# Weight sums and differences of a seven-product down projection, formed on GpSimd instead of VectorE

## The chip, the cores and the metric

The kernel runs on one core of one Trainium2 chip. The metric is the time of one execution on the device in microseconds; the kernel before takes 2917.14 us (median of 3 runs, 2915.57 to 2918.15). All names and lines below are those of the kernel before.

## The reference, cut to what matters

One decoder layer on 512 tokens of width 2048, in float32: three token mixers, a gated merge, an output projection and a squared-ReLU MLP of width 8192. The change lies in the second matrix product of the MLP:

```python
h2 = rms_norm(x, mlp_norm_w[l])
x = x + jnp.square(jax.nn.relu(h2 @ w_mlp_up[l])) @ w_mlp_down[l]
```

`w_mlp_down` is 8192 x 2048 in float32.

## The kernel before, in words

**Matrix products in three passes.** A float32 tile is split into a high part, rounded to the type that TensorE multiplies (fp32r), and the rest. `wsplit` (lines 110 to 115) does that for a weight tile `raw` of 128 partitions x 1024 elements: ScalarE casts it to `whi` (L112), then VectorE subtracts to get `wlo` (L114). `mm3` (lines 122 to 125) issues three matmuls for each product: high with high, high with rest, rest with high. There are four buffers for `raw` (`RAWS = 4`) and three each for `whi` and `wlo`.

**The MLP in eight slices.** The 8192 hidden channels go in eight slices of 1024 (`NE = 8`). For a slice, `up_steps` forms the hidden activations `u` (accumulators `fa`): 16 weight tiles, 24 matmuls each. `down_units` multiplies them with the slice's rows of `w_mlp_down` and adds the result into `x1` (accumulators `da`). For seven of the eight slices it does so by seven products of quarter matrices instead of eight (Strassen's scheme, the table `SEVEN`): each product takes one quarter or a sum or difference of two quarters of the activations, the same of the weights, and its result is added to one or two quarters of the output (L1001, on VectorE, reading `da` from PSUM). Of the seven products five take a sum or difference of two weight quarters, in the table's order the first three and the last two; the fourth and fifth take one quarter as it is.

**The step.** `merged_order` alternates one step of the next slice's up projection with one step of this slice's down projection. A step of the pair, as the text calls it, is thus one up tile (called U; 24 matmuls) and one down unit: half the columns of one product, which is two weight tiles (called A and B here, `i = 0` and `i = 1`; 12 matmuls each). A slice has 14 such steps: 6 with paired weights, 4 with single ones, 4 with paired ones; the two up tiles left over follow, so that three up tiles stand in a row there. Seven slices have 70 steps with paired weights, and 140 sums.

**A paired weight tile.** Both quarters come by DMA into two `raw` buffers (L988, 512 KB each, queue of SyncE). L991 adds the second to the first in place; then the tile goes through `wsplit`:

```python
for k0, m0, _ in bt:
    raw = wp.tile([P, 2, 512], F32, tag="raw", bufs=RAWS, name="raw")
    nc.sync.dma_start(out=raw, in_=rows(w_dn, e_ * 1024 + k0 * 512 + i * 256, m0 * 1024 + c * 512, 512))
    raws.append(raw)
if len(bt) == 2:
    nc.vector.tensor_tensor(out=raws[0], in0=raws[0], in1=raws[1], op=sgn[bt[1][2]][0])
hi, lo = wsplit(raws[0], 512)
```

The second buffer of a pair is free when the sum is done, the first when `wlo` is. A paired step so takes five `raw` buffers of a ring of four: one for U (L104), two for A, two for B. SyncE issues the transfers in the order U, A, A, B, B; each waits until its buffer has been read.

**The order of the work.** Each engine runs its instructions in a fixed order that a scheduler sets when the program is built; an instruction that waits holds all behind it on its engine or queue.

Of the kernel before, what the change touches and what calls it, by code (L numbers as in the profile page):

```python
# [49 lines left out]
def tile_layer(ctx: ExitStack, tc: tile.TileContext, a, out: bass.AP):  # L50
    nc = tc.nc
# [9 lines left out]
    def T(name, dt=F32, shape=(P, 512)):  # L61
        return big.tile(list(shape), dt, tag="T", bufs=N_SLOTS, name=name)
# [4 lines left out]
    def sm(name, shape=(P, 512)):  # L67
        return psm.tile(list(shape), F32, tag="sm", name=name)
# [41 lines left out]
    def wsplit(raw, n):  # L110
        hi = wp.tile([P, 2, n], F32R, tag="whi", bufs=3, padded_shape=[P, 2, 512], name="whi")
        nc.scalar.copy(out=hi, in_=raw)  # L112
        lo = wp.tile([P, 2, n], F32R, tag="wlo", bufs=3, padded_shape=[P, 2, 512], name="wlo")
        nc.vector.tensor_tensor(out=lo, in0=raw, in1=hi.bitcast(F32), op=ALU.subtract)  # L114
        return hi, lo

    def rows(w, k0, c0, n):
        return w[k0:k0 + 2 * P, c0:c0 + n].rearrange("(k p) c -> p k c", p=P)
# [3 lines left out]
    def mm3(ps, l_hi, l_lo, r_hi, r_lo, first, last):  # L122
        nc.tensor.matmul(ps, lhsT=l_hi, rhs=r_hi, start=first, stop=False)  # L123
        nc.tensor.matmul(ps, lhsT=l_hi, rhs=r_lo, start=False, stop=False)  # L124
        last_mm[0] = nc.tensor.matmul(ps, lhsT=l_lo, rhs=r_hi, start=False, stop=last)  # L125
# [721 lines left out]
    for h in range(NH):  # L847
# [3 lines left out]
        raws = []  # L851
# [85 lines left out]
    sgn = {1: (ALU.add, r2), -1: (ALU.subtract, nr2)}  # L937
# [24 lines left out]
    def split(src):  # L962
        hh = T("a_h", F32R, (P, 2, 256))
        hl = T("a_l", F32R, (P, 2, 256))
        nc.scalar.copy(out=hh, in_=src)  # L965
        nc.vector.tensor_tensor(out=hl, in0=src, in1=hh.bitcast(F32), op=ALU.subtract)
        return hh, hl

    def down_units(e_, u):

        for at, bt, ct in SEVEN:
            act = []
            for i in range(2):
                t0, k0, _ = at[0]
                src = u[2 * k0 + i, t0]
                if len(at) == 2:
                    t1, k1, s1 = at[1]
                    both = T("a_s", shape=(P, 2, 256))
                    nc.vector.tensor_tensor(out=both, in0=src, in1=u[2 * k1 + i, t1], op=sgn[s1][0])
                    src = both  # L980
                act.append(split(src))
            for c in range(2):
                accs = [sm("da") for _ in range(2)]
                for i in range(2):
                    raws = []
                    for k0, m0, _ in bt:
                        raw = wp.tile([P, 2, 512], F32, tag="raw", bufs=RAWS, name="raw")
                        nc.sync.dma_start(out=raw, in_=rows(w_dn, e_ * 1024 + k0 * 512 + i * 256, m0 * 1024 + c * 512, 512))  # L988
                        raws.append(raw)
                    if len(bt) == 2:  # L990
                        nc.vector.tensor_tensor(out=raws[0], in0=raws[0], in1=raws[1], op=sgn[bt[1][2]][0])  # L991
                    hi, lo = wsplit(raws[0], 512)
                    ah, al = act[i]
                    for t in range(2):
                        for k in range(2):
                            cs = slice(t * P, (t + 1) * P)
                            mm3(accs[t], ah[:, k, cs], al[:, k, cs], hi[:, k, :], lo[:, k, :], i == 0 and k == 0, i == 1 and k == 1)
                for t in range(2):
                    for t0, m0, s0 in ct:
                        tt, cc_ = 2 * t0 + t, 2 * m0 + c  # L1000
                        nc.vector.scalar_tensor_tensor(out=x1[tt, cc_], in0=accs[t], scalar=sgn[s0][1][:, tt:tt + 1], in1=x1[tt, cc_], op0=ALU.mult, op1=ALU.add)  # L1001
                yield
# [12 lines left out]
    for e_ in range(NE - 1):  # L1015
        nu = {}
        merged_order(up_steps(e_ + 1, nu), down_units(e_, u))
        u = nu
# [81 lines left out]
```

## Time and profile before

| what | value |
|---|---|
| median of 3 runs | 2917.14 us (2915.57 to 2918.15) |
| profiled execution: its own time | 2913.22 us |
| profiled execution: span of the instructions | 2911.4 us |
| granted TensorE clock, mean | 0.998 of full speed |
| TensorE busy with matmuls | 2880.4 us, 99% of the span |
| VectorE busy | 1569.0 us, 54% |
| ScalarE busy | 1016.0 us, 35% |
| GpSimd busy | 125.1 us, 4% |

The profiled execution's own time is 1.8 us over its span. Shares of busy time are means over stages with different limits; the MLP with the seven products lies from about 1667 to 2808 us, and there the shares are others. Idle time of an engine costs something only where TensorE comes to wait for it.

### The profile page before, as it was taken

Reading aid. Unit: us, or ns where it says so; the run is one execution under the profiler, and the core shown is the slowest. Engines: PE = TensorE matmul, PEld = TensorE weight load, DVE = VectorE, ACT = ScalarE, POOL = GpSimd, SP = SyncE. Lnnn points to the kernel's source line nnn. Section 1 sums busy time; section 2 is a strip of 40 time slices with the busy share of each in tenths; the row PEclk is TensorE's granted clock in tenths of the full one; section 3 lists DMA queues with packets and bytes.
Section 4 is the critical chain, followed back from the end, with each engine's and each line's share of the span. In section 5 each row is a group of like instructions: output and inputs, shape, how many; then the busy total and the mean of one; then the engine's idle time right before and its main releaser. Section 6 shows DMA issues by size and latency. Waiting matters only on the chain.

```text
span 2911.4 us, 34617 instructions
## 1 busy us (share of the span) xinstructions
PE 2880.4 (99%) x13710; PEld 2341.0 (80%) x13710; DVE 1569.0 (54%) x2194; ACT 1016.0 (35%) x1606; POOL 125.1 (4%) x134
## 2 busy tenths in 40 slices
PE   8999999999999999999999999999999999999999
PEld 6988777777888888888888888787888878788887
DVE  5435665645223233333332377767777677777753
ACT  6333434334222222222232333333434333343431
POOL 0001111100000010000000000000000000000000
PEclk9999999999999999999999999999999999999999
DMA  6423222222333333333333366656666666656653
GB/s 230 115 73 89 68 64 71 57 56 59 101 94 97 99 94 101 95 95 100 123 110 103 120 210 209 212 181 209 192 204 204 208 217 196 209 184 210 192 181 109
DMA packets 259773, 403.47 MB, mean 139 GB/s; under 512 B 23159, under 2 KB 80282, under 8 KB 259610
## 3 DMA queue, kind: packets, MB, share of 16 engines
q1 hardware_dynamic: 250240, 398.61, 44.3%
q10 hardware_dynamic: 9370, 2.64, 0.4%
q8 instruction: 107, 1.75, 0.2%
q14 instruction: 56, 0.46, 0.1%
HBM read 396.60 MB, written 4.60 MB: 138 GB/s over the span
## 4 chain that ended last, share of the span: by engine, by line
PE 87%; DVE 5%; DMA 5%; ACT 1%; issue 1%; POOL 1%; SPq 0%; ACTq 0%; DVEq 0%; POOLq 0%
PE fa L123 19%; PE fa L125 19%; PE fa L124 19%; PE da L124 6%; PE da L125 6%; PE da L123 5%; DMA raw<-in_w_mlp_down_dram 4%; PE ta L123 2%; PE ta L124 2%; PE ta L125 2%; DVE wlo L114 2%; DVE raw L991 2%; DVE x L1001 1%; PE dps L807 1%; PE ps L814 1%
## 5 line engine op out<-in xcount | busy, mean ns | idle before, releaser
L114 DVE TENSOR_TENSOR wlo<-raw,whi 128x1024 fp32r<-128x1024 f32 (+2 forms) x604 | 723.2, 1205 | 909.5 <-ACT whi L112 906.4
L112 ACT CAST whi<-raw 128x1024 fp32r<-128x1024 f32 (+2 forms) x604 | 621.9, 1035 | 1434.6 <-PE fa L124 709.2
L123 PE MATMUL fa<-h_h,whi 128*128 128x512 f32 x2336 | 928.0, 397 | 0.0
L125 PE MATMUL fa<-h_h,wlo 128*128 128x512 f32 x2336 | 913.6, 391 | 2.7 <-DVE wlo L114 2.6
L124 PE MATMUL fa<-h_l,whi 128*128 128x512 f32 x2336 | 912.8, 391 | 0.0
L123 PEld LDWEIGHTS fa<-h_h,whi 128*128 128x128 f32 x2336 | 438.8, 188 | 97.9 <-issue 11.3
L125 PEld LDWEIGHTS fa<-h_h,wlo 128*128 128x128 f32 x2336 | 438.7, 188 | 97.2 <-DVE wlo L114 5.3
L124 PEld LDWEIGHTS fa<-h_l,whi 128*128 128x128 f32 x2336 | 439.1, 188 | 86.6 <-issue 1.2
L124 PE MATMUL da<-wlo,a_h 128*128 128x512 f32 x912 | 358.9, 393 | 7.9 <-DVE wlo L114 7.8
L123 PE MATMUL da<-whi,a_h 128*128 128x512 f32 x912 | 355.4, 390 | 0.2
L125 PE MATMUL da<-whi,a_l 128*128 128x512 f32 x912 | 355.1, 390 | 0.0
L991 DVE TENSOR_TENSOR raw<-raw 128x1024 f32<-128x1024 f32 x140 | 171.2, 1223 | 174.2 <-DMA raw<-in_w_mlp_down_dram 174.0
L124 PEld LDWEIGHTS da<-wlo,a_h 128*128 128x128 f32 x912 | 171.2, 188 | 54.5 <-DVE wlo L114 19.7
L123 PEld LDWEIGHTS da<-whi,a_h 128*128 128x128 f32 x912 | 171.3, 188 | 36.9 <-ACT a_h L965 1.0
L125 PEld LDWEIGHTS da<-whi,a_l 128*128 128x128 f32 x912 | 171.3, 188 | 34.4
L1001 DVE SCALAR_TENSOR_TENSOR x<-da,r,x 128x512 f32<-128x512 f32 x280 | 195.7, 742 | 0.2 <-PE da L125 0.2
L123 PE MATMUL ta<-whi,m_h 128*128 128x512 f32 x256 | 99.9, 390 | 0.0
L125 PE MATMUL ta<-whi,m_l 128*128 128x512 f32 x256 | 99.7, 389 | 0.0
L124 PE MATMUL ta<-wlo,m_h 128*128 128x512 f32 x256 | 99.7, 389 | 0.0
L123 PE MATMUL fa<-ob_h,whi 128*128 128x512 f32 x256 | 99.6, 389 | 0.0
L124 PE MATMUL fa<-ob_l,whi 128*128 128x512 f32 x256 | 99.6, 389 | 0.0
L125 PE MATMUL fa<-ob_h,wlo 128*128 128x512 f32 x256 | 99.6, 389 | 0.0
(286 smaller groups left out, 2114.2 us busy)
## 6 DMA issues: line engine op xcount, KB each, us to landing
raw<-in_w_mlp_down_dram SPq DMA_DIRECT2D x352, 512.0 KB, 4.1
raw<-in_w_mlp_up_dram SPq DMA_DIRECT2D x128, 512.0 KB, 3.8
raw<-in_w_in_dram SPq DMA_DIRECT2D x112, 512.0 KB, 3.6
raw<-in_w_in_dram SPq DMA_DIRECT2D x120, 256.0 KB, 3.0
raw<-in_w_out_dram SPq DMA_DIRECT2D x32, 512.0 KB, 3.8
raw<-in_w_mem_kv_dram SPq DMA_DIRECT2D x16, 512.0 KB, 4.2
raw<-in_p_swa_dram SPq DMA_DIRECT2D x12, 512.0 KB, 3.8
raw<-in_p_dn_dram SPq DMA_DIRECT2D x12, 512.0 KB, 3.9
```

What stands on the lines that cost most here:

```text
L112: nc.scalar.copy(out=hi, in_=raw)
L114: nc.vector.tensor_tensor(out=lo, in0=raw, in1=hi.bitcast(F32), op=ALU.subtract)
L123: nc.tensor.matmul(ps, lhsT=l_hi, rhs=r_hi, start=first, stop=False)
L124: nc.tensor.matmul(ps, lhsT=l_hi, rhs=r_lo, start=False, stop=False)
L125: last_mm[0] = nc.tensor.matmul(ps, lhsT=l_lo, rhs=r_hi, start=False, stop=last)
L807: nc.tensor.matmul(dps[rs, :], lhsT=R[rs, t, :], rhs=tmp, start=True, stop=True)
L814: nc.tensor.matmul(ps2, lhsT=kd[rs, t, :], rhs=delta, start=True, stop=True)
L991: nc.vector.tensor_tensor(out=raws[0], in0=raws[0], in1=raws[1], op=sgn[bt[1][2]][0])
L1001: nc.vector.scalar_tensor_tensor(out=x1[tt, cc_], in0=accs[t], scalar=sgn[s0][1][:, tt:tt + 1], in1=x1[tt, cc_], op0=ALU.mult, op1=ALU.add)
```

## The change

L991, the sum or difference of two weight tiles, is issued on GpSimd instead of VectorE. Operands, shapes and order in the program's text stay.

```diff
--- before.py
+++ after.py
@@ -988,7 +988,7 @@
                         nc.sync.dma_start(out=raw, in_=rows(w_dn, e_ * 1024 + k0 * 512 + i * 256, m0 * 1024 + c * 512, 512))
                         raws.append(raw)
                     if len(bt) == 2:
-                        nc.vector.tensor_tensor(out=raws[0], in0=raws[0], in1=raws[1], op=sgn[bt[1][2]][0])
+                        nc.gpsimd.tensor_tensor(out=raws[0], in0=raws[0], in1=raws[1], op=sgn[bt[1][2]][0])
                     hi, lo = wsplit(raws[0], 512)
                     ah, al = act[i]
                     for t in range(2):
```

On GpSimd all 140 sums stand in a row at the end of its program, behind the merge's last additions:

```order
 L894 TENSOR_TENSOR mg<-mg,sg 128x512 x32
+L991 TENSOR_TENSOR raw<-raw 128x1024 x140
 L1096 UNCONDITIONAL_BRANCH
```

Nothing else is issued there in the MLP, so a sum waits on GpSimd only for its own data.

On VectorE, in the paired steps late in a slice, the sums stood between the subtractions and the additions to `x1`. `wlo_15950` and `wlo_15971` are the rests of an A and a B tile, `wlo_15991` that of the next U:

```order
-L991 TENSOR_TENSOR raw_15943<-raw_15943,raw_15945 128x1024
+L114 TENSOR_TENSOR wlo_15950<-raw_15943,whi_15948 128x1024
 L1001 SCALAR_TENSOR_TENSOR x1_11397<-da_15865,r2_11993,x1_11397 128x512
-L114 TENSOR_TENSOR wlo_15950<-raw_15943,whi_15948 128x1024
 L1001 SCALAR_TENSOR_TENSOR x1_11399<-da_15866,r2_11993,x1_11399 128x512
-L991 TENSOR_TENSOR raw_15964<-raw_15964,raw_15966 128x1024
 L114 TENSOR_TENSOR wlo_15971<-raw_15964,whi_15969 128x1024
-L991 TENSOR_TENSOR raw_16031<-raw_16031,raw_16033 128x1024
 L114 TENSOR_TENSOR wlo_15991<-raw_15987,whi_15989 128x1024
```

The sums are gone from the row, and the subtractions keep their order among themselves.

On the queue of SyncE the transfers keep their order, and some waits change the engine whose counter they watch. 15943 and 15945 are the two quarters of an A tile, 15964 and 15966 those of its B tile, 15987 the next U, 16031 and 16033 the next A:

```order
-L988 DMA raw_15943<-in_w_mlp_down_dram 128x2x512 [waits DMAHW1_49,DVE_49]
+L988 DMA raw_15943<-in_w_mlp_down_dram 128x2x512 [waits DMAHW1_49,Pool_49]
 L988 DMA raw_15945<-in_w_mlp_down_dram 128x2x512 [waits DVE_49]
 L988 DMA raw_15964<-in_w_mlp_down_dram 128x2x512 [waits DVE_49]
-L988 DMA raw_15966<-in_w_mlp_down_dram 128x2x512 [waits DMAHW6_49,DMAHW2_49,DVE_49]
-L104 DMA raw_15987<-in_w_mlp_up_dram 128x2x512 [waits DMAHW4_49,DVE_49]
-L988 DMA raw_16031<-in_w_mlp_down_dram 128x2x512 [waits DMAHW0_49,DVE_49]
-L988 DMA raw_16033<-in_w_mlp_down_dram 128x2x512 [waits DMAHW6_49,DVE_49]
+L988 DMA raw_15966<-in_w_mlp_down_dram 128x2x512 [waits DMAHW6_49,DMAHW4_49,Pool_49]
+L104 DMA raw_15987<-in_w_mlp_up_dram 128x2x512 [waits DMAHW2_49,DVE_49]
+L988 DMA raw_16031<-in_w_mlp_down_dram 128x2x512 [waits DMAHW6_49,DMAHW0_49,Pool_49]
+L988 DMA raw_16033<-in_w_mlp_down_dram 128x2x512 [waits DVE_49]
```

The second quarter of B and the first quarter of the next A now wait for a sum on GpSimd (`Pool_49`); the second quarter of A stands right behind the first and waits for a subtraction.

## Rows read from the trace of the kernel before

**Rows 1.** The page, busy time of each engine.
```profile
PE 2880.4 (99%) x13710; PEld 2341.0 (80%) x13710; DVE 1569.0 (54%) x2194; ACT 1016.0 (35%) x1606; POOL 125.1 (4%) x134
```
**Rows 2.** Windows, the MLP's paired stage: PE, PEld, DVE, ACT, POOL busy, clock, DMA.
```profile
1667.00:2808.00 1141.00, 1130.34 (x4946) 925.08 (x4945) 841.30 (x939) 425.02 (x552) 0.00 (x0) 1.00 0.64 203
```
**Rows 3.** Groups of instructions in that stage: busy, mean ns, idle before.
```profile
L114 DVE TENSOR_TENSOR wlo<-raw,whi 128x1024 fp32r<-128x1024 f32 x305 | 367.7, 1220 | 125.7 <-ACT whi L112 124.2
...
L112 ACT CAST whi<-raw 128x1024 fp32r<-128x1024 f32 x303 | 315.7, 1052 | 610.9 <-DVE raw L991 389.8 <-PE fa L124 126.7 <-PE da L125 82.5
...
L991 DVE TENSOR_TENSOR raw<-raw 128x1024 f32<-128x1024 f32 x137 | 167.6, 1223 | 160.8 <-DMA raw<-in_w_mlp_down_dram 160.7
```
**Rows 4.** Waits in that stage: total us, times, longest.
```profile
DVE raw L991 <- DMA raw<-in_w_mlp_down_dram: 160.7, 102, 3.7
...
PE da L124 <- DVE wlo L114: 7.8, 10, 1.3
```
**Rows 5.** Waits of SyncE's DMA queue in that stage.
```profile
SPq L988 <- DVE raw L991: 106.4, 94, 1.7
```
**Rows 6.** Timeline of VectorE, four paired steps: start, length, what, idle before.
```profile
2099.59 1.23 DVE L991 TENSOR_TENSOR raw<-raw 128x1024 f32<-128x1024 f32 x1 [1.80 <-DMA raw<-in_w_mlp_down_dram]
...
2118.88 1.23 DVE L991 TENSOR_TENSOR raw<-raw 128x1024 f32<-128x1024 f32 x1 [2.36 <-DMA raw<-in_w_mlp_down_dram]
...
2124.14 1.23 DVE L991 TENSOR_TENSOR raw<-raw 128x1024 f32<-128x1024 f32 x1 [0.29 <-DMA raw<-in_w_mlp_down_dram]
...
2130.28 1.23 DVE L991 TENSOR_TENSOR raw<-raw 128x1024 f32<-128x1024 f32 x1 [2.50 <-DMA raw<-in_w_mlp_down_dram]
...
2151.62 1.23 DVE L991 TENSOR_TENSOR raw<-raw 128x1024 f32<-128x1024 f32 x1 [3.60 <-DMA raw<-in_w_mlp_down_dram]
```
**Rows 7.** Timeline of SyncE's queue beside them.
```profile
2120.14 0.37 SPq L988 DMA_DIRECT2D raw<-in_w_mlp_down_dram  x1
...
2122.56 0.37 SPq L988 DMA_DIRECT2D raw<-in_w_mlp_down_dram  x1
...
2125.39 0.37 SPq L988 DMA_DIRECT2D raw<-in_w_mlp_down_dram  x1
```
**Rows 8.** Timeline of TensorE: first matmuls of steps (`fa`) and of a down unit (`da`).
```profile
2100.29 0.39 PE L123 MATMUL fa<-h_h,whi 128*128 128x512 f32 x1
...
2111.17 0.39 PE L123 MATMUL fa<-h_h,whi 128*128 128x512 f32 x1
...
2160.13 0.39 PE L123 MATMUL da<-whi,a_h 128*128 128x512 f32 x1
```
**Rows 9.** Timeline of VectorE, early paired steps of another slice.
```profile
1867.16 1.22 DVE L991 TENSOR_TENSOR raw<-raw 128x1024 f32<-128x1024 f32 x1 [1.49 <-DMA raw<-in_w_mlp_down_dram]
...
1878.17 1.23 DVE L991 TENSOR_TENSOR raw<-raw 128x1024 f32<-128x1024 f32 x1 [1.33 <-DMA raw<-in_w_mlp_down_dram]
```
**Rows 10.** Timeline of TensorE there: first matmuls of two steps.
```profile
1867.23 0.39 PE L123 MATMUL fa<-h_h,whi 128*128 128x512 f32 x1
...
1878.38 0.39 PE L123 MATMUL fa<-h_h,whi 128*128 128x512 f32 x1
```
**Rows 11.** The `raw` tile's view in that stage, transfers from issue to landing.
```profile
DMA to landing us min/median/max: 3.6/4.1/6.1
```
**Rows 12.** GpSimd's groups over the whole span: busy, mean ns.
```profile
L701 POOL TENSOR_TENSOR craw<-craw,cc 128x256 f32<-128x256 f32 x6 | 4.4, 726 | 0.0
```
**Rows 13.** Timeline of GpSimd in the merge, two additions of the same shape.
```profile
1205.94 1.29 POOL L894 TENSOR_TENSOR mg<-mg,sg 128x512 f32<-128x512 f32 x1 [53.80 <-DVE sg L893]
...
1211.34 2.26 POOL L894 TENSOR_TENSOR mg<-mg,sg 128x512 f32<-128x512 f32 x1
```
**Rows 14.** Timeline of VectorE beside the second of them.
```profile
1210.15 0.68 DVE L893 TENSOR_TENSOR sg<-fa,sg 128x512 f32<-128x512 f32 x1
1210.76 1.71 DVE L114 TENSOR_TENSOR wlo<-raw,whi 128x1024 fp32r<-128x1024 f32 x1
1212.38 2.60 DVE L899 TENSOR_TENSOR m_l<-mg,m_h 128x512 fp32r<-128x512 f32 x2
```

## The prediction

> **What bounds the kernel now.** I read the page first: TensorE is busy 99% of the span [rows 1], so a change can only cost or give back what TensorE waits. The windows narrow that to the stage of the change, 1141 us in which VectorE is busy 841.30 us (74%), GpSimd not at all, and TensorE idles 1141.00 - 1130.34 = 10.7 us [rows 2]. That is about all there is to win.
>
> Then I asked what TensorE is close to waiting for. The groups of VectorE show that the sums (L991, 1.22 us each) sit idle 160.8 us before them, waiting for weights [rows 3]: 102 of the 137 sums that the trace holds there come as soon as their data land [rows 4]. The queue's waits show the other half: 94 times a transfer waits for a sum to free its buffer [rows 5]. Sum and transfer wait for each other: a loop. The timelines let one measure it. The sum of an A tile starts at 2118.88 and is done at 2120.11 [rows 6]; at 2120.14 SyncE issues the second quarter of B into the buffer that it freed [rows 7]; the sum of B starts at 2124.14, ends at 2125.37, and at 2125.39 the second quarter of the next A leaves, whose sum starts at 2130.28 [rows 6, 7]. One turn is 11.40 us: two sums (2.46) and two transfers with their handoffs (4.03 and 4.91). In the early steps of another slice it is 1878.17 - 1867.16 = 11.01 us [rows 9]. I take 11.2.
>
> TensorE needs 2111.17 - 2100.29 = 10.88 us for a step [rows 8]. So the loop is already a little slower than TensorE in paired steps. It hardly shows, because the tiles are ahead at the start of a run of paired steps and the lead is used up slowly; where it is used up the steps stretch to the loop (11.15 us, from the starts of two steps) [rows 10].
>
> **The change, part by part.**
>
> *Taken from VectorE:* 140 sums of 1.22 us, 171 us, and their waiting at the head of VectorE's row. Worth little: VectorE delays TensorE by a few us in all (7.8 us in ten waits for `wlo`) [rows 4].
>
> *Put on GpSimd:* 140 sums of 128x1024. The trace has no such shape on GpSimd. The nearest rows: 0.73 us for 128x256 [rows 12] and 1.29 us for 128x512 with nothing beside it [rows 13], so 0.56 us for every 256 more, and 1.29 + 2 x 0.56 = 2.41 us. Bounds: 1.22 us would need a GpSimd as fast as VectorE, which the 1.29 us for half the size rules out, so the lower end is the slope's 2.41 too; the upper one is twice 1.29 = 2.58. I take 2.41, from the slope of two rows.
>
> The Trainium skill puts a price on it too: "GPSIMD Engine Reference", section on performance versus the Vector engine, gives 4497 ns on GpSimd and 2293 ns on VectorE for 2048 elements; half of that, an estimate, is 2.25 us. By it the loop below is 0.32 us shorter and the time 3030 us; no run here shows that size.
>
> *The loop:* both its sums grow by 2.41 - 1.22 = 1.19, so 11.2 + 2.38 = 13.6 us. Nothing hides this: a sum starts when its data land and its end releases the next transfer. The queue's order stays, and behind a transfer that waits for GpSimd stand U and both A tiles.
>
> *The A pair:* its first quarter left at 2122.56, 2.83 us ahead of the second [rows 7]. Now it waits for the sum of B too, and both leave together. Between nothing and 2.0 us more (longest less median landing, 6.1 - 4.1) [rows 11]; I take 0.5, since only the tail of one transfer's data has to pass first.
>
> *GpSimd beside VectorE:* a `wlo` that met an addition on GpSimd took 1.71 us instead of 1.22, two `m_l` 2.60 us, and the addition between them 2.26 instead of 1.29 [rows 13, 14]. With both operands in SBUF one engine waits until the other is through. The VectorE product that reads PSUM kept its 0.68 us beside GpSimd [rows 14], so L1001 should not hold a sum. A sum can be held by nothing or by a whole `wlo`, 1.22 us, twice a turn: 0 to 2.4. In a turn of 14 us VectorE has three `wlo`, 3.7 us [rows 3], a quarter of the time; half an instruction is 0.6, so 0.15 for each sum: I take 0.3 a turn.
>
> Sum: 13.6 + 0.5 + 0.3 = 14.4 us a turn, 3.5 over TensorE's step. Bounds: 11.0 + 2.38 = 13.4 (2.5 over) and, all upper ends at once, 11.4 + 2 x 1.36 (a sum of 2.58) + 2.0 + 2.4 = 18.5.
>
> *The lead that is spent first.* Before a run of four (the last two products), the sum of the first B starts at 2099.59 [rows 6]; TensorE needs that tile three quarters into the step that starts at 2100.29 [rows 8], at 2108.45: 8.86 later. From that go the sum (2.41), cast and subtraction (1.05 + 1.22) [rows 3], handoffs (0.2) and the 1.2 by which the sum of A ahead is longer: 2.8 us of lead. Before a run of six, with three up tiles in a row ahead, the sum of B starts at 2151.62 [rows 6] and is needed 2.72 after the unit's start at 2160.13 [rows 8]: 11.2 later, a lead of 5.1. The single products between are fed without sums and give the lead back.
>
> A run of four has three turns behind its first: 3 x 3.5 - 2.8 = 7.7 us late. A run of six: 5 x 3.5 - 5.1 = 12.4. Per slice 20.1, seven slices 141 us. TensorE already loses 10.7 of this stage, which lie in the same place: +130 us. On the profiled execution that is 2913.2 + 130 = 3043; the median of the runs lies 3.9 us above that execution, so **3047 us**.
>
> **The rivals.**
>
> *Faster.* VectorE at 74% no longer stands at the head of its row waiting for weights, subtractions come on time, and TensorE's 10.7 us come back: 2906 us. The Trainium skill points this way with a caveat: "Perfetto Trace Analysis", section on optimizing Scalar and DVE operations, says that offloading to GpSimd may make sense where VectorE is saturated, but may not help since the two share a read port. For it: GpSimd is idle [rows 2]. Against it: this needs a loop of no more than 10.88, so a sum of (10.88 - 8.74) / 2 = 1.07 us with its waits; half the size took 1.29 [rows 13]. Chance 0.04.
>
> *Slower by the shared operands.* Every sum meets a whole `wlo`: 14.1 + 2.4 = 16.5 us a turn, 5.6 over; 14.0 + 22.9 = 37 us a slice, 259 - 11 = +248: 3165 us. For it: in the merge nearly every meeting cost a hold [rows 13, 14]. The Trainium skill, "SBUF — State Buffer", section on who interferes with whom, calls it an exclusive lock for the whole instruction, and the trace agrees (1.71 us against 1.22). Against it: a landing falls at no fixed place in VectorE's row, and the subtractions of a tile come after its own sum. Chance 0.12.
>
> *The lead covers most.* Transfers land at their shortest, 3.6 us [rows 11], because the queue runs less full: 2 x 2.41 + 2 x 3.6 + 0.1 = 12.1 a turn, 1.2 over; 0.8 + 0.9 = 1.7 a slice, 12 - 11 = +1: about 2918, and anything up to 2980 if only some of them do. Against it: 4.03 and 4.91 were measured where the queue was waiting, not full. Chance 0.10.
>
> *The sums don't move, or GpSimd does something else there.* The order shows all 140 on GpSimd and none left on VectorE. Then 2917; chance 0.01.
>
> **How the numbers follow.** The forecast has 0.73. My range is 2980 to 3130: its low end is the low loop (2.5 over: 4.7 + 7.4 = 12.1 a slice, 85 - 11 = +74, 2991) and a little of the third rival, its high end a turn of 15.9 (5.0 over: 12.2 + 19.9 = 32 a slice, +214); it leaves out the first and the last rival, most of the third and half of the second, some 0.18. About 0.2% (6 us) is what a measurement can tell from no change. Faster by more: 0.04. Within: 0.03 of the third rival and the last, 0.04. Slower: the rest, 0.92.
>
> **What would show it.** In the profile of the changed kernel: sums on GpSimd of about 2.4 us, mostly released by the landing of `raw`; one paired turn, from an A sum to the next, of 13.5 to 15 us; TensorE waiting for `wlo` or `whi` of the B tiles, up to 140 us in the stage and almost none in the single steps; the stage longer by as much, and nothing outside it. It is wrong if the turn stays near 11 us, if TensorE's waiting lies in single steps too, or if VectorE's subtractions rather than landings release what TensorE waits for.

## The result, and the profile after

The changed kernel takes 3110.64 us (median; 3106.34 to 3112.04). The kernel before, run beside it, takes 2917.3 us (2915.57 to 2918.15). The ratio is 1.0661, with a 95% interval of 1.0643 to 1.068: 193 us slower. The forecast was slower by 130, 3047 us, with a range of 2980 to 3130. The direction and the place were right and the time lies inside the range; the size of the step, 193 instead of 130, was not right.

The page of the changed kernel, busy time of each engine, answers to [rows 1]. VectorE gave up 129 us, GpSimd took 343, and the matmuls are the same in number:

```profile
PE 2953.0 (95%) x13710; PEld 2372.6 (76%) x13710; DVE 1439.6 (46%) x2054; ACT 1014.0 (33%) x1606; POOL 468.2 (15%) x274
```

The paired stage is now 1330 us long instead of 1141 [rows 2]. Windows, same columns: TensorE idles 129.3 us, its granted clock is 0.96 instead of 1.00, and the DMA share falls from 0.64 to 0.54. The three further windows are a run of six without its first step, the single steps behind it, and a run of four behind those. In the single steps TensorE is busy 54.40 of 54.40 us at full clock; the whole loss lies in the paired steps.

```profile
1667.00:2997.00 1330.00, 1200.66 (x4932) 956.01 (x4930) 705.30 (x795) 420.13 (x549) 335.21 (x137) 0.96 0.54 173
...
1856.00:1931.60 75.60, 63.18 (x241) 48.63 (x240) 35.81 (x42) 17.77 (x19) 21.91 (x10) 0.91 0.54 176
1931.60:1986.00 54.40, 54.40 (x241) 45.05 (x240) 39.84 (x47) 23.03 (x33) 7.17 (x3) 1.00 0.54 171
1986.00:2030.70 44.70, 37.10 (x146) 28.74 (x145) 16.05 (x17) 10.18 (x10) 12.30 (x6) 0.93 0.56 177
```

The groups of that stage answer to [rows 3]. A sum takes 2452 ns on average, 2.0 times the 1223 of VectorE, and waits 994.7 us in all for its data. The subtractions of weight tiles kept their 1222 ns: in this kernel none of them is held. What is held are the rests of the activations on VectorE (L966; one form takes 1023 ns on average where the kernel before has 685, the other 895 where it has 686, together 28 us) and 16 of the 140 sums (some 8 us).

```profile
L114 DVE TENSOR_TENSOR wlo<-raw,whi 128x1024 fp32r<-128x1024 f32 x300 | 362.1, 1222 | 579.4 <-ACT whi L112 578.9
...
L991 POOL TENSOR_TENSOR raw<-raw 128x1024 f32<-128x1024 f32 x137 | 335.9, 2452 | 999.8 <-DMA raw<-in_w_mlp_down_dram 994.7 <-DVE x L1001 5.1
```

The waits name the loop. 136 of 137 sums are released by a landing, where it was 102 [rows 4]; 123 transfers wait for a sum, where it was 94 [rows 5]; and TensorE waits for the high parts of the down tiles, and another 40.4 us for their low parts (the last fence is SyncE's queue):

```profile
POOL raw L991 <- DMA raw<-in_w_mlp_down_dram: 994.7, 136, 43.6
...
PE da L123 <- ACT whi L112: 86.1, 47, 3.1
```
```profile
SPq L988 <- POOL raw L991: 319.3, 123, 3.6
```

**One steady turn**, from GpSimd's timeline, SyncE's queue and TensorE's first matmuls of steps:

```profile
1804.17 2.39 POOL L991 TENSOR_TENSOR raw<-raw 128x1024 f32<-128x1024 f32 x1 [5.66 <-DMA raw<-in_w_mlp_down_dram]
1811.08 2.35 POOL L991 TENSOR_TENSOR raw<-raw 128x1024 f32<-128x1024 f32 x1 [4.51 <-DMA raw<-in_w_mlp_down_dram]
1819.22 2.39 POOL L991 TENSOR_TENSOR raw<-raw 128x1024 f32<-128x1024 f32 x1 [5.79 <-DMA raw<-in_w_mlp_down_dram]
```
```profile
1806.60 0.37 SPq L988 DMA_DIRECT2D raw<-in_w_mlp_down_dram  x1
1807.06 0.41 SPq L104 DMA_DIRECT2D raw<-in_w_mlp_up_dram  x1
...
1813.45 0.37 SPq L988 DMA_DIRECT2D raw<-in_w_mlp_down_dram  x1
1813.87 0.46 SPq L988 DMA_DIRECT2D raw<-in_w_mlp_down_dram  x1
```
```profile
1803.58 0.39 PE L123 MATMUL fa<-h_h,whi 128*128 128x512 f32 x1
...
1820.03 0.39 PE L123 MATMUL fa<-h_h,whi 128*128 128x512 f32 x1
...
1833.29 0.39 PE L123 MATMUL fa<-h_h,whi 128*128 128x512 f32 x1
```

The sum of A ends at 1806.56; 0.04 us later the second quarter of B leaves, U right behind it; the sum of B starts 4.51 us after A's end. It ends at 1813.43, both quarters of the next A leave at 1813.45 and 1813.87, and the sum starts 5.79 after. One turn is 1819.22 - 1804.17 = 15.05 us: 4.74 for two sums and 10.30 for two transfers with their handoffs, which took 8.94 before. TensorE's two steps there take 16.45 and 13.26 us, 14.9 on average, against 10.88.

**What the change moved besides.** The four `raw` buffers are given out when the program is built, and with the sums on GpSimd they went to other tiles. Counted in the two programs, a quarter of B waits for the sum of A in all 70 paired steps of the changed kernel, but in only 35 of the kernel before; in the other 35 the next U takes the buffer that this sum frees. So the half of the loop from the sum of A to the sum of B was closed in half of the steps before and is closed in all of them after. The turn of [rows 9] is one where it was open: U leaves behind the sum of A that ends at 1868.38 (SyncE's queue of the kernel before), and the sum of B, at 1872.07, follows a subtraction in VectorE's row without a wait. Its 11.01 us are as long as the loop measured beside it, but they are not that loop.

```profile
1868.41 0.37 SPq L104 DMA_DIRECT2D raw<-in_w_mlp_up_dram  x1
```

### The profile page after: what moved, and what is told of

Read it like the earlier page. It is cut to its first block, busy times and chain, and to the rows that moved or that the text cites. A ratio compares the mean times of both kernels' runs of the same rounds, so it can differ in the third digit from the quotient of the medians.

```text
span 3104.5 us, 34614 instructions
## 1 busy us (share of the span) xinstructions
PE 2953.0 (95%) x13710; PEld 2372.6 (76%) x13710; DVE 1439.6 (46%) x2054; ACT 1014.0 (33%) x1606; POOL 468.2 (15%) x274
## 4 chain that ended last, share of the span: by engine, by line
PE 62%; DMA 20%; POOL 11%; DVE 2%; ACT 2%; issue 1%; SPq 1%; POOLq 0%; ACTq 0%; DVEq 0%
DMA raw<-in_w_mlp_down_dram 20%; PE fa L123 14%; PE fa L124 14%; PE fa L125 14%; POOL raw L991 10%; PE da L124 2%; PE da L125 2%; PE da L123 2%; PE ta L125 2%; PE ta L123 2%; PE ta L124 2%; DVE wlo L114 1%; ACT whi L112 1%; SPq L988 1%; PE dps L807 1%
## 5 line engine op out<-in xcount | busy, mean ns | idle before, releaser
L991 POOL TENSOR_TENSOR raw<-raw 128x1024 f32<-128x1024 f32 x140 | 343.1, 2451 | 1260.9 <-DMA raw<-in_w_mlp_down_dram 1255.8
L123 PEld LDWEIGHTS fa<-h_h,whi 128*128 128x128 f32 x2336 | 440.5, 189 | 102.0 <-issue 11.3
L123 PE MATMUL da<-whi,a_h 128*128 128x512 f32 x912 | 378.2, 415 | 87.3 <-ACT whi L112 87.2
L124 PE MATMUL da<-wlo,a_h 128*128 128x512 f32 x912 | 382.6, 420 | 41.1 <-DVE wlo L114 41.1
L125 PE MATMUL da<-whi,a_l 128*128 128x512 f32 x912 | 373.9, 410 | 0.0
L123 PEld LDWEIGHTS da<-whi,a_h 128*128 128x128 f32 x912 | 181.0, 198 | 147.6 <-ACT whi L112 108.7
L124 PEld LDWEIGHTS da<-wlo,a_h 128*128 128x128 f32 x912 | 182.7, 200 | 99.7 <-DVE wlo L114 62.0
L125 PEld LDWEIGHTS da<-whi,a_l 128*128 128x128 f32 x912 | 183.0, 201 | 37.3
L1001 DVE SCALAR_TENSOR_TENSOR x<-da,r,x 128x512 f32<-128x512 f32 x280 | 195.1, 743 | 0.0
L894 POOL TENSOR_TENSOR mg<-mg,sg 128x512 f32<-128x512 f32 x32 | 49.6, 1579 | 639.6 <-DVE sg L893 639.6
```

The source lines that it names most:

```text
L894: nc.gpsimd.tensor_tensor(out=merged[kt], in0=merged[kt], in1=sg[j], op=ALU.add)
L991: nc.gpsimd.tensor_tensor(out=raws[0], in0=raws[0], in1=raws[1], op=sgn[bt[1][2]][0])
```

## The experiments

**Theory 1:** the time is set by a loop through buffers and queue order (sum, transfer, sum, transfer), and a longer sum lengthens the turn. **Theory 2, its rival:** GpSimd and VectorE hold each other at the operands that they share, and the holds make the loss. In the rows below L992 is L991 and L989 is L988 where the edit added a line.

### 1. Half a sum on GpSimd

```diff
-nc.gpsimd.tensor_tensor(out=raws[0], in0=raws[0], in1=raws[1], ...)
+nc.gpsimd.tensor_tensor(out=raws[0][:, :, 0:256], in0=raws[0][:, :, 0:256], in1=raws[1][:, :, 0:256], ...)
```

> The changed kernel with each sum on GpSimd cut to half of its columns; the other half of each second weight quarter is left out of the products. Theory 1 (a loop of two sums and two bunched transfers through the raw buffers): a sum takes some 1.3 us, a turn 15.05 - 2 x 1.1 = 12.85 us instead of 15.05, 2.2 us saved on about eight turns a slice, 193 - 7 x 17.5 = 70 us over the kernel before: 2970 to 3010. Theory 2 (GpSimd and VectorE hold each other at the shared operands, and the holds, not the length of the sum, make the loss): as many meetings, so most of the loss stays: 3070 to 3110.

Measured: 2978.84 us, ratio 1.021 (1.0195 to 1.0226). GpSimd's timeline in a run of four:

```profile
1790.94 1.29 POOL L991 TENSOR_TENSOR raw<-raw 128x512 f32<-128x512 f32 x1 [5.71 <-DMA raw<-in_w_mlp_down_dram]
1797.06 1.29 POOL L991 TENSOR_TENSOR raw<-raw 128x512 f32<-128x512 f32 x1 [4.82 <-DMA raw<-in_w_mlp_down_dram]
1804.25 1.29 POOL L991 TENSOR_TENSOR raw<-raw 128x512 f32<-128x512 f32 x1 [5.91 <-DMA raw<-in_w_mlp_down_dram]
```

The turn is 13.31 us here; steady turns run from 12.2 to 13.7. The gaps between sums (4.82 and 5.91 here) stayed what they were; only the sums shrank. That is theory 1. It also says that the longer gaps belong to which transfers leave together, not to the length of the sum. And it parts the loss: these sums are nearly as long as VectorE's (1.29 us against 1.22), and in this program too a quarter of B waits for the sum of A in all 70 steps; yet 62 us are lost. So, as an estimate, some 62 of the 193 us go with which transfer waits for which sum and some 130 with the length of the sum; the two were not varied apart.

### 2. Two sums in a row on VectorE

```diff
 nc.vector.tensor_tensor(out=raws[0], in0=raws[0], in1=raws[1], ...)
+nc.vector.tensor_tensor(out=raws[0], in0=raws[0], in1=raws[1], ...)
```

> The kernel before with every sum issued twice on VectorE, so the second quarter is added twice; GpSimd does nothing there. Theory 1 (only the length of the sum in the loop counts, not its engine): the pair of sums takes 2.45 us, as long as one on GpSimd, so the turn is again near 15 us and the time 3080 to 3140, and as TensorE's waits lie in the same steps. Theory 2 (the loss comes from GpSimd beside VectorE): no GpSimd here, so only VectorE's own 171 us more at 74% busy: 2920 to 2960.

Measured: 3011.63 us, ratio 1.0323 (1.0306 to 1.034): 95 us slower, between the two forecasts. 2.45 us of sums without GpSimd cost far more than theory 2's 3 to 43 us, but half of what they cost on GpSimd. The run is no clean comparison: the scheduler gave the buffers out in another order, in which U rather than a quarter of B waits for the sum of A in 55 of the 70 paired steps, and moved matmuls of the paired steps. So it shows only that a long sum costs much without GpSimd.

### 3 and 4. Own buffers for second quarters, with the sums on GpSimd and on VectorE

```diff
-N_SLOTS = 75
+N_SLOTS = 71
...
-raw = wp.tile([P, 2, 512], F32, tag="raw", bufs=RAWS, name="raw")
+tg, nb = ("raw2", 2) if raws else ("raw", RAWS)
+raw = wp.tile([P, 2, 512], F32, tag=tg, bufs=nb, name="raw")
```

> The changed kernel with two raw buffers more, kept for second quarters alone (the staging slots go from 75 to 71 to make room). A second quarter then waits for the sum of the same half one step earlier, not for the sum just before it, and a first quarter for a subtraction: the loop that runs through both sums of a step is open, though the sums on GpSimd stay at 2.4 us. Theory 1: the steps go back to 10.9 to 11.2 us, time 2905 to 2940. Theory 2: the sums and subtractions hold each other as before, time 3070 to 3110. Rival 3 (GpSimd's sum as plain latency ahead of the cast and subtraction, without a loop): some 1.2 us on every B tile, 3000 to 3080.

> The kernel before, sums on VectorE, with the same own buffers for second quarters. Theory 1: its own loop (11.2 us against a step of 10.88) is open too, so up to 10.7 us that TensorE idles in this stage come back: 2900 to 2915. Theory 2: no GpSimd, no change: 2914 to 2920. If the 71 slots cost something elsewhere, both buffer kernels are slower than this outside the stage.

Measured: with the sums on GpSimd 2958.74 us, ratio 1.0146 (1.0131 to 1.0161); with the sums on VectorE 2894.62 us, ratio 0.9919 (0.9903 to 0.9936). The second is faster than both kernels of this study. Windows of it, the paired stage: TensorE is busy 1123.00 of 1123.00 us; from the second step on each takes 10.88 us.

```profile
1667.00:2790.00 1123.00, 1123.00 (x4957) 929.88 (x4956) 839.28 (x939) 428.90 (x554) 0.00 (x0) 1.00 0.64 205
```

So the loop of the kernel before was worth 22 us. With GpSimd the same buffers took back 152 of the 193 us: the runs of four are at 10.88 again, but most steps of a run of six take 12 to 16 us. GpSimd's timeline in a run of six, and then SyncE's queue beside it:

```profile
1861.56 4.76 POOL L992 TENSOR_TENSOR raw<-raw 128x1024 f32<-128x1024 f32 x2 [8.53 <-DMA raw<-in_w_mlp_down_dram]
1874.60 4.75 POOL L992 TENSOR_TENSOR raw<-raw 128x1024 f32<-128x1024 f32 x2 [8.28 <-DMA raw<-in_w_mlp_down_dram]
```
```profile
1866.35 0.37 SPq L989 DMA_DIRECT2D raw<-in_w_mlp_down_dram  x1
...
1867.43 0.37 SPq L989 DMA_DIRECT2D raw<-in_w_mlp_down_dram  x1
```

Both sums of a step now run back to back, end at 1866.32, and three transfers leave behind that end; the next sum starts 8.28 us later: a turn of 13.04. The order of the queue says why (12895 and 12897 are the first and second quarter of an A tile, 12916 and 12918 of its B):

```
L989 DMA raw_12897<-in_w_mlp_down_dram 128x2x512 [waits DMAHW2_49,Pool_49]
L104 DMA raw_12851<-in_w_mlp_up_dram 128x2x512 [waits DMAHW0_49,DVE_49]
L989 DMA raw_12918<-in_w_mlp_down_dram 128x2x512 [waits DMAHW4_49,DMAHW1_49,Pool_49]
L989 DMA raw_12895<-in_w_mlp_down_dram 128x2x512 [waits DMAHW3_49,DVE_49]
L989 DMA raw_12916<-in_w_mlp_down_dram 128x2x512 [waits DMAHW7_49,DVE_49]
```

A's first quarter (12895) waits for a subtraction only, but stands behind B's second quarter (12918), which waits for a sum on GpSimd. A loop of two sums and one transfer was left, through the queue. But 64 us lay between the two runs, and theory 2 could still claim them.

### 5. The control for the slots

The kernel before with `N_SLOTS = 71`.

> The kernel before with 71 staging slots instead of 75 and nothing else: a control for the runs with more raw buffers. If slots cost or give nothing, 2914 to 2921; if the gain of 22 us came from them, about 2895.

Measured: 2918.01 us, ratio 1.0002 (0.9991 to 1.0012). The slots give and cost nothing; the 22 us are the buffers'.

### 6 and 7. GpSimd in the runs of six alone, and in the runs of four alone

```diff
-nc.gpsimd.tensor_tensor(out=raws[0], ...)
+(nc.gpsimd if bt in [s[1] for s in SEVEN[:3]] else nc.vector).tensor_tensor(out=raws[0], ...)
```

and `SEVEN[5:]` in the other.

> GpSimd forms the sums of the first three products of a slice only (the run of six paired steps); those of the last two (the run of four) stay on VectorE. Theory 1a (the run of six began late in the changed kernel because the run of four ahead of it, with two up tiles between, had already used up the lead): with the run of four on VectorE the lead of 5.1 us is there, 5 turns x 4.17 - 5.1 = 15.8 us a slice instead of 22.2, less some 20 us that the kernel before loses there anyway: +90, 2995 to 3020. Theory 1b (the run of six is slow by itself, by VectorE's activation work at its start): it stays at 22 us a slice, +135: 3040 to 3065.

> The other half: GpSimd forms the sums of the last two products only (the run of four). Theory 1a: its own 8.7 us a slice (+61) and the lead that it takes from the run of six behind it, whose sums on VectorE have little slack (11.2 us a turn against 10.88): +65 to +100, 2980 to 3015, and the steps after the two up tiles are longer than in the kernel before. Theory 1b: the run of four alone, +45 to +61: 2962 to 2980. Under 1a the two halves alone add up to less or more than 193 as their leads interact; under 1b they add up to 193.

Measured: 3044.18 us, ratio 1.0438 (1.0418 to 1.0457), and 2988.99 us, ratio 1.0245 (1.0228 to 1.0261): +126 and +71, together 198 against 193. My explanation 1a, that the run of four had eaten the lead of the run of six, fell: with the run of four on VectorE the run of six is still 19.5 to 22.7 us late a slice (18.0 in the first). The run of six is late by itself, as 1b said. The second run fits 1b less well: 2989 lies above its 2962 to 2980 and inside the range of 1a. By the starts of its steps the run of four alone is 9.9 us late a slice, and the run of six behind it 3.6 instead of 2.4, so a small part does pass from one to the other. But the long first turns are there without GpSimd too. TensorE's and VectorE's timelines of the kernel before, at the start of a run of six:

```profile
2165.57 0.39 PE L123 MATMUL fa<-h_h,whi 128*128 128x512 f32 x1
...
2177.64 0.39 PE L123 MATMUL fa<-h_h,whi 128*128 128x512 f32 x1
```
```profile
2158.97 1.22 DVE L991 TENSOR_TENSOR raw<-raw 128x1024 f32<-128x1024 f32 x1 [3.32 <-DMA raw<-in_w_mlp_down_dram]
2166.00 1.23 DVE L991 TENSOR_TENSOR raw<-raw 128x1024 f32<-128x1024 f32 x1 [1.13 <-DMA raw<-in_w_mlp_down_dram]
...
2170.98 2.35 DVE L114 TENSOR_TENSOR wlo<-raw,whi 128x1024 fp32r<-128x1024 f32 x2
...
2176.35 1.23 DVE L991 TENSOR_TENSOR raw<-raw 128x1024 f32<-128x1024 f32 x1 [0.68 <-DMA raw<-in_w_mlp_down_dram]
...
2182.47 1.22 DVE L991 TENSOR_TENSOR raw<-raw 128x1024 f32<-128x1024 f32 x1
```

From the A sum at 2158.97 to the next at 2176.35 are 17.4 us, not 11.2. And TensorE's step behind the three up tiles takes 2177.64 - 2165.57 = 12.07 us, 1.2 over; in the other five such places it is 1.1 to 1.6 over. From one B sum to the next it is 14.38 us (2151.62 [rows 6] to 2166.00) and then 16.47. The 1.2 us are not the wait of a sum for its data: the sum of that A tile ends at 2160.19, but its cast on ScalarE stands behind activation work and starts at 2168.99, and its subtraction stands behind four additions on VectorE (L1001) and starts at 2170.98. The same place in the changed kernel (GpSimd's timeline, SyncE's queue, and TensorE's first matmul of the run of six):

```profile
1837.18 2.40 POOL L991 TENSOR_TENSOR raw<-raw 128x1024 f32<-128x1024 f32 x1 [8.95 <-DMA raw<-in_w_mlp_down_dram]
1844.43 2.94 POOL L991 TENSOR_TENSOR raw<-raw 128x1024 f32<-128x1024 f32 x1 [4.86 <-DMA raw<-in_w_mlp_down_dram]
1853.56 2.92 POOL L991 TENSOR_TENSOR raw<-raw 128x1024 f32<-128x1024 f32 x1 [6.18 <-DMA raw<-in_w_mlp_down_dram]
1862.41 2.38 POOL L991 TENSOR_TENSOR raw<-raw 128x1024 f32<-128x1024 f32 x1 [5.94 <-DMA raw<-in_w_mlp_down_dram]
1872.34 2.40 POOL L991 TENSOR_TENSOR raw<-raw 128x1024 f32<-128x1024 f32 x1 [7.54 <-DMA raw<-in_w_mlp_down_dram]
1878.87 2.36 POOL L991 TENSOR_TENSOR raw<-raw 128x1024 f32<-128x1024 f32 x1 [4.14 <-DMA raw<-in_w_mlp_down_dram]
```
```profile
1864.82 0.37 SPq L104 DMA_DIRECT2D raw<-in_w_mlp_up_dram  x1
1865.29 0.92 SPq L988 DMA_DIRECT2D raw<-in_w_mlp_down_dram  x2
```
```profile
1850.56 0.39 PE L123 MATMUL da<-whi,a_h 128*128 128x512 f32 x1
```

From A sum to A sum two turns of 16.38 and 18.78 us, from B sum to B sum 17.98 and 16.46. In the second turn between A sums, three transfers (U and both quarters of A) leave behind the one sum that ends at 1864.79, and the next sum starts 7.54 us later.

### 8 and 9. Three buffers for up tiles and first quarters, four for second quarters

As in 3 and 4, with `RAWS = 3`, four buffers `raw2` and `N_SLOTS = 69`; the sums on GpSimd, and as a control on VectorE.

> All sums on GpSimd; three raw buffers for up tiles and first quarters and four buffers of their own for second quarters (slots 75 to 69 for room). In the run with two such buffers the first quarter of the next A tile still stood in SyncE's queue behind a second quarter that waits for the sum of B, so a loop of two sums and one transfer, some 13 us, was left in the run of six. Here no first quarter stands behind a transfer that waits for the other half's sum: the longest loop is one sum, one cast, one subtraction and one transfer, 2.4 + 1.05 + 1.22 + 5 + handoffs, some 10 us. Theory 1 (loops alone): all steps near 10.88, 2895 to 2925. Theory 2 (the 64 us that the run with two such buffers lost against the same buffers with sums on VectorE are GpSimd and VectorE holding each other): as many meetings, 2945 to 2970.

> The control for the run with three buffers for up tiles and first quarters and four for second quarters: the same with the sums on VectorE. If the 57 us that that run lost against the kernel before came from having only three buffers for three kinds of tile, this one loses as much: 2950 to 2980 (Theory 1). If they came from the sums on GpSimd (Theory 2), this one is at 2893 to 2917.

Measured: 2974.56 us, ratio 1.0195 (1.0179 to 1.0211), and on VectorE 2928.83, ratio 1.0036 (1.0023 to 1.0049). The first fits theory 2; the control lies between the two: three buffers for three kinds of tile cost some 10 us against the kernel before, the sums on GpSimd some 46 more. By the starts of the steps a run of six is 7.1 to 9.5 us late a slice with GpSimd and 4.5 to 5.7 with VectorE, nearly all of it in its first steps, and the run of four behind it up to 2.8 and 0. But the pair doesn't decide between the theories, because its premise fails. In SyncE's queue of the first program the first quarter of A still stands behind a transfer that waits for the sum of the B tile just before it, in 61 of 69 places: the loop of two sums and one transfer was left here too. And here a hold does lie on the way to TensorE, at the start of a run of six (VectorE's and TensorE's timelines of the run with the sums on GpSimd):

```profile
1859.10 2.88 DVE L966 TENSOR_TENSOR a_l<-a_s,a_h 128x512 fp32r<-128x512 f32 x1
1862.01 2.78 DVE L979 TENSOR_TENSOR a_s<-u 128x512 f32<-128x512 f32 x1
```
```profile
1868.61 0.50 PE L124 MATMUL da<-wlo,a_h 128*128 128x512 f32 x1 [3.87 <-DVE wlo L114]
```

Two sums in a row on GpSimd, from 1858.85 to 1864.24, hold two VectorE instructions to 2.88 and 2.78 us instead of 0.69 each, and the subtraction for which TensorE waits 3.87 us stands behind them, at 1867.35. How much of the 46 us goes with the loop and how much with such holds was not separated; the next run asks the same with four buffers.

### 10. Second quarters on GpSimd's own queue

The kernel of run 3, with one more edit: the second quarters are issued by GpSimd, right behind the sum that frees their buffer.

```diff
-nc.sync.dma_start(out=raw, in_=rows(w_dn, ...))
+(nc.gpsimd if raws else nc.sync).dma_start(out=raw, in_=rows(w_dn, ...))
```

> All sums on GpSimd, two buffers of their own for second quarters (as in the first run of that kind), and the second quarters issued by GpSimd itself, right behind the sum that frees their buffer; SyncE's queue carries up tiles and first quarters, and no transfer in it waits for a sum. The loop of two sums and one transfer that queue order had left is gone, with four buffers for the rest. Theory 1 (what was left of the loss, 64 us over the same buffers with sums on VectorE, came from queue order): most of it goes, 2895 to 2925, unless an issue on GpSimd costs it more than some 1 us, which lengthens each sum's turn. Theory 2 (GpSimd and VectorE hold each other, no loop): 2945 to 2970 again.

Measured: 2914.49 us, ratio 0.998 (0.9971 to 0.999): all sums on GpSimd, and no slower than the kernel before. And yet here the holds are at their worst. First the groups of the stage, then VectorE's timeline in a run of six (GpSimd's sum beside it takes 3.42 us), last what TensorE waits for in the stage:

```profile
L114 DVE TENSOR_TENSOR wlo<-raw,whi 128x1024 fp32r<-128x1024 f32 x305 | 526.0, 1734 | 228.6 <-ACT whi L112 228.0
L992 POOL TENSOR_TENSOR raw<-raw 128x1024 f32<-128x1024 f32 x136 | 344.3, 2532 | 656.3 <-DMA raw<-in_w_mlp_down_dram 642.5 <-DVE x L1002 11.0 <-DVE wlo L114 1.2
```
```profile
1855.66 2.79 DVE L114 TENSOR_TENSOR wlo<-raw,whi 128x1024 fp32r<-128x1024 f32 x1 [0.54 <-ACT whi L112]
```
```profile
PE fa L123 <- ACT whi L112: 5.8, 6, 1.5
PE fa L125 <- DVE wlo L114: 5.5, 6, 0.9
```

A subtraction takes 1734 ns on average instead of 1222, 0.51 x 305 = 156 us of holds, where the changed kernel had none on its subtractions and some 37 us elsewhere. TensorE waits 11.3 us in all, nearly all in the first two steps of a run of six; the others are at 10.88 or within 0.4 of it. **Theory 2 falls as the cause of the 193 us:** there is far more holding here, and the loss is gone. (That holds can cost where they lie on TensorE's way, run 8 shows.) What holds, issues and the longer sum cost together in these buffers is the 20 us between this run and run 4.

### 11. The loop closed again in that kernel

```diff
-tg, nb = ("raw2", 2) if raws else ("raw", RAWS)
+tg, nb = ("raw2", 1) if raws else ("raw", RAWS)
```

> The run whose second quarters are issued by GpSimd, with one buffer for second quarters instead of two and nothing else changed: each second quarter now leaves when the sum just before it is done, so sum, transfer, sum, transfer is a closed loop again, while up tiles and first quarters still leave early on SyncE's queue, and only one transfer waits for each sum. Theory 1 (the closed loop costs, whatever queue it runs through): two sums of 2.4, two issues some 0.3 after a sum's end, two transfers that land alone, 4.0 to 4.9: a turn of 13.4 to 15.2, most likely 13.8; 5 x 2.9 + 3 x 2.9 - 2.8 us a slice, some 20 x 7 = 140 less the 22 of the kernel before: 3005 to 3060. A turn of 13.8 would say that the 1.3 us over my forecast in the changed kernel came from transfers that left together; one of 15 that it didn't. Theory 2 (only holds between GpSimd and VectorE): 2910 to 2920, as with two buffers.

Measured: 3041.0 us, ratio 1.0411 (1.0391 to 1.0431). One buffer fewer costs 127 us. GpSimd's timeline:

```profile
1800.39 2.38 POOL L992 TENSOR_TENSOR raw<-raw 128x1024 f32<-128x1024 f32 x1 [3.86 <-DMA raw<-in_w_mlp_down_dram]
1803.07 0.72 POOL L989 DMA_DIRECT2D raw<-in_w_mlp_down_dram  x1 [0.30 <-POOL raw L992]
1807.37 2.37 POOL L992 TENSOR_TENSOR raw<-raw 128x1024 f32<-128x1024 f32 x1 [3.58 <-DVE x L1002]
...
1814.49 2.38 POOL L992 TENSOR_TENSOR raw<-raw 128x1024 f32<-128x1024 f32 x1 [3.73 <-DMA raw<-in_w_mlp_down_dram]
```

The turn is 14.10 us. The gaps between sums are 4.60 and 4.75, together 9.35, where the changed kernel had 10.30; the issue comes 0.30 us after the sum instead of 0.04, so without that delay it would be 8.83, about the 8.94 of the kernel before. Most of the run's gaps lie between 4.6 and 5.2. With one transfer behind each sum the extra gap of the changed kernel is gone. (The releaser named at 1807.37 is an addition on VectorE; the sum needs only its two quarters.)

### 12. An attempt at the same without GpSimd's queue

The changed kernel with `RAWS = 3` and one buffer `raw2` for second quarters (the other edit as in 3).

> The changed kernel with its four raw buffers divided in three for up tiles and first quarters and one for second quarters; no buffer is added. Each second quarter waits for the sum just before it, so the loop still runs through both sums, but a first quarter waits for a subtraction and can leave earlier: the two quarters of an A tile need not leave together behind one sum. Theory 1 with the price of bunched transfers (a turn of 2 x 2.39 and two transfers of 4.5 and 5.8): the turn falls towards 2 x 2.39 + 4.0 + 4.9 = 13.7, some 8 x 1.3 us a slice, -75: 3020 to 3060. If bunching is not what made the transfers long, the turn stays at 15: 3095 to 3125.

Measured: 3125.71 us, ratio 1.0702 (1.0686 to 1.0718). The steady gaps stayed near those of the changed kernel, from 4.1 to 5.0 and from 5.5 to 6.8. It doesn't speak on bunching: the queue put A's second quarter, which waits for the sum of B, ahead of A's first, so both left together again. Run 11 took its place.

## Why the prediction was right, and where its size was wrong

*What bounds the kernel (a loop of sums and transfers):* right for the changed kernel. Runs 4, 10 and 11 open it, open it with the sums on GpSimd, and close it again: 2895, 2914 and 3041 us. For the kernel before it was read too widely: the loop through both sums was closed in 35 of 70 paired steps, and the turn of [rows 9] is not one of them. That the change would close it in all 70 was not foreseen; the sum of the forecast counts a closed loop in every steady turn, and so was right there in part by luck.

*"10.7 us is about all there is to win":* too low. Run 4 won 22. By the starts of its steps the kernel before is 20.6 us late in this stage. TensorE's idle time shows less: a matmul's row lasts 0.39 us though the next starts 0.23 behind it, so the first 0.16 us of each wait count as busy, and the first matmul behind a wait has a row of 0.50. In the changed kernel TensorE's busy time grew by 2953.0 - 2880.4 = 72.6 us with the same matmuls; some 41 of these are matmuls at the lower clock (last section).

*A sum of 2.41 us:* right, 2.39 measured where nothing holds it. The Trainium skill's "GPSIMD Engine Reference", section on performance versus the Vector engine, gives 2.25 as an estimate, by half of its figure for twice the size; the trace's 2.39 decides.

*The A pair, 0.5 us for leaving together:* **too small.** The transfers of a turn took 10.30 instead of 8.94, 1.36 more; this term was mis-sized. U leaves 0.46 us behind B's second quarter and both quarters of A leave 0.42 apart, so two transfers share each gap; with one in each gap (run 11) the 1.36 are not there.

*GpSimd beside VectorE, 0.3 us a turn:* too large for the steady turn, where it is nothing (2.39 and 2.35): the sum, the cast and the subtraction of a tile follow one another, and the loop keeps them apart. The Trainium skill, "SBUF — State Buffer", section on who interferes with whom, calls it an exclusive lock, and the runs agree where the two are seen to meet (2.94 us for a sum at 1844.43 above, 2.79 for a subtraction in run 10). But a hold costs only where something waits for it.

*The turn:* 15.05 instead of 14.4, 4.17 over TensorE's step instead of 3.5.

*The run of four, a lead of 2.8:* right. 3 x 4.17 - 2.8 = 9.7; by the starts of the steps it is 8.3 to 12.0 us late a slice, 9.4 on average.

*The run of six, five steady turns less a lead of 5.1:* **the count of the turns was the step that failed.** The trace has 20.2 to 22.4 us late, 21.5 on average, in the six slices where three up tiles stand ahead; the forecast was 12.4. With the measured turn it would be 5 x 4.17 - 5.1 = 15.8. The lead was there, somewhat smaller: the first B tile is ready 3.5 to 5.3 us before TensorE needs it, 4.0 on average (in the slice shown its sum ends at 1847.37, cast, subtraction and handoffs take 2.4, and TensorE needs it 2.72 behind 1850.56). But the turns behind it are not five steady ones. From B sum to B sum the first two take 17.5 and 17.1 us on average and only the other three 15.1, together 25.5 over TensorE's steps; 25.5 - 4.0 = 21.5 is what the trace has. The kernel before shows it: its first two turns there take 14.4 and 16.4 us, not 11.2. The first slice, whose run of six stands behind the up projection alone, has the same long turns, a lead of some 9 us, and is 16.5 late.

By terms, from the forecast's +130: the turn, 0.65 x 8 x 7 = 36; the two long turns of each run of six, 25.5 - 5 x 4.17 = 4.6, times 7, 32; the 20.6 instead of 10.7 that the kernel before loses itself, -10. That makes 188, where 193 were measured; the 5 us left lie in the leads and between the runs. These are shares of the lateness that the trace shows, not effects tried one by one.

*The rivals:* a faster kernel was ruled out by the loop, as said. The lock on every sum would have meant sums of 3.6 us; the mean was 2.45. Transfers didn't land sooner on a less crowded queue, as the third rival had it; they landed later, with a median of 4.5 us instead of 4.1.

## What to carry to other kernels

An operation that stands between a landing and the release of the buffer that the next transfer needs counts with its full length, however idle its engine is; once the loop is open (a buffer of its own for what only that operation reads, and no early transfer queued behind a late one), the engine counts for little: 2895 us with the sums on VectorE and 2914 on GpSimd, where the two kernels of this study have 2917 and 3111. Look at what a queue puts behind a waiting transfer, not only at buffers: the same two buffers gave 2959 us on SyncE's queue and 2914 on two queues. Moving an operation can also move buffers: count in the new program which transfer waits for which operation before the old loop is carried over. And before steady turns are counted behind a lead, measure the first turns of a run in the kernel before; here they took 14.4 and 16.4 us where the steady ones took 11.

## What the runs showed of the hardware that was not expected

Transfers of 512 KB that leave together behind one sum land late together: in the turns shown, from the first issue to the start of the sum that needs the data it is 4.3 to 4.5 us with one (run 11), 4.5 to 5.8 with two (the steady turn), and 7.5 to 8.3 with three (the start of the run of six, and run 3). A transfer issued by GpSimd occupies it for 0.72 us and starts 0.30 us behind the sum, where SyncE's starts 0.04 behind it.

The granted clock of paired stretches is 0.91 and 0.93 of 2.4 GHz where single steps have 1.00, so part of them runs at 1.2 GHz. In the changed kernel TensorE had waited 2.65 us at 1814.56 and 0.76 us more behind that; from 1816.5 to 1819.5 its granted clock is 0.50 (windows, then TensorE's timeline):

```profile
1816.50:1819.50 3.00, 3.00 (x8) 2.34 (x7) 0.40 (x1) 0.00 (x0) 0.28 (x1) 0.50 0.95 367
```
```profile
1818.66 0.63 PE L125 MATMUL da<-whi,a_l 128*128 128x512 f32 x1
1819.09 0.63 PE L123 MATMUL da<-whi,a_h 128*128 128x512 f32 x1
```

There a matmul takes 0.63 us instead of 0.39, and the next starts 0.43 behind it instead of 0.23. The changed kernel has 203 such matmuls, some 41 us in all, and the kernel before none. Most of them stand ahead of another wait of the same run; whether they cost anything beyond the loop's own time was not tried by itself.
